# Four modulation vectors of layer 1 as VectorE sums in place of TensorE products

## The chip, the cores and the metric

The kernel runs on one core of a Trainium2 chip. Its time is the device time of one launch in microseconds (us), taken as the median of several executions. A separate execution was recorded by the hardware profiler; rows with times come from it. The engines are PE (TensorE, matrix products; PEld loads its stationary operands), DVE (VectorE), ACT (ScalarE), POOL (GpSimd) and SP (SyncE, which issues most DMAs). Each of them runs its own list of instructions in order, and semaphores tie the lists together.

## What is computed

Two layers over 512 latent tokens and 256 context tokens, D = 1024. Six modulation vectors per layer come from the condition `c` (and six from `c_ctx`); they shift, scale and gate the two halves of the layer:

```python
for layer in range(DEPTH):
    mod_x = silu_c @ ada_w[layer] + ada_b[layer]
    mod_c = silu_cc @ ada_w[layer] + ada_b[layer]
    sh1, sc1, g1, sh2, sc2, g2 = [m[:, None, :] for m in jnp.split(mod_x, 6, axis=-1)]
    ...
    hx = modulate(rmsnorm(x, norm1_g[layer]), sh1, sc1)
    ...
    x = x + g1 * (mx @ w_out[layer])
    hx = modulate(rmsnorm(x, norm2_g[layer]), sh2, sc2)
    x = x + g2 * squared_relu_mlp(hx, w_mlp1[layer], w_mlp2[layer])
```

The mixer that gives `mx` is four heads of bidirectional retention and four of gated linear attention behind one input projection; the output projection is `w_out`. Context tokens go through the same weights in layer 1.

## The kernel before, in words

**Products.** All float32 products of weights and activations are made of three float32r products (`mm3`, L437 to L439): high part by high part, high by low, low by high. A weight slab of 128 x 1024 comes by one DMA of 512 KB into one of four raw buffers (`NRAW = 4`), ACT makes its high part (L244), DVE its low part (L245), and up to `NSPL = 6` split slabs live at once. The raw buffers are shared by the slabs of the projections (`raw_wi`, `raw_wo`, `raw_wob`, `raw_m`) and the slabs of `ada_w` (`adaw`).

**What sets the order.** The program is a list of items. For the mixer it is written by hand in `SCHEDULE`, 25 lines, each with a projection block and the attention stages that run behind it. The items are emitted one after the other, and at each one `ch.tick()` emits the next step of every chain under way (norms, residuals, evacuations). No engine leaves this order afterwards.

**The modulation vectors.** Numbered u = 0 to 5 (sh1, sc1, g1, sh2, sc2, g2), 1024 features each, for two conditions. Layer 1's u = 0 and 1 are made on PE in quarters at the start. Its u = 2 to 5 are made on PE in 16 steps of `ada_step` (L279 to L292), in two groups g of 2048 features and eight k tiles each; one step stands after each slab block of `SCHEDULE`, from its first line on, until the 16 are done. A step loads two slabs and makes four fp32 products, 32 columns by 512. `ada_finish` then copies the rows out, transposes them on PE (four transposes of 128 x 128 per group) and adds the bias on DVE. Layer 2's six vectors are made another way, by `ada_sums` (L324 to L353), during layer 1's MLP: per k tile two DVE instructions, one per condition, add slab times scalar to a sum of 128 x 1024 (L340 for the first k tile, L342 for the other seven); after eight k tiles eight small products with a column of ones (L348) add up the partitions, and two transposes of 128 x 128 follow.

**The output projection of layer 1.** `wo0` to `wo7` for token group 0 (512 columns), then `wo6b`, `wo7b`, `wo0b`, ... in the order `second` for token group 1 (256 columns). In the traces their PSUM tiles are `pwo`, by the program's names pwo_j_g. After each, DVE adds the gated product to the residual stream `x` (L535), ACT squares it and DVE adds the square to the norm's sum (L473). While group 1 is projected, the second norm is applied to group 0: `xn` and `yl` on DVE (L517, L521, L515), `yh` on ACT, `xn` of two tiles on POOL (L510). Before the projection, `reload` lets POOL issue eight DMAs that bring `x` back into SBUF. The MLP follows.

Of the kernel before, what the change touches and what calls it, by code (L numbers as in the profile page):

```python
# [16 lines left out]
P = 128  # L17
# [22 lines left out]
class Item:  # L40
    """A piece of the program: emits instructions; may need weight slabs; a stage runs one block after its deps."""
# [5 lines left out]
class Chains:  # L47
    """Instruction chains that hop between engines: each tick emits the next step of every chain under way.

    Queued chains start one per tick, with at most WIDTH of them under way."""  # L50
# [45 lines left out]
class Act:  # L96
    """A moving operand in two float32r parts, made by chains for token ranges."""
# [10 lines left out]
# one block of projections and the attention stages that run behind it, per line; at most NSLOT tiles live  # L108
# [30 lines left out]
def build(ctx: ExitStack, tc, a):  # L139
# [7 lines left out]
    tp = ctx.enter_context(tc.tile_pool(name="tab", bufs=1))  # L147
    mp = ctx.enter_context(tc.tile_pool(name="mp", bufs=NSLOT))
# [23 lines left out]
    def bc(col, n):  # L172
        """[P, c] -> [P, c, n], each value repeated n times."""
        return col.rearrange("p (c o) -> p c o", o=1).to_broadcast([col.shape[0], col.shape[1], n])

    def rep(tab, c):
        """[P, n] -> [P, c, n], the row repeated c times."""
        return tab.rearrange("p (o t) -> p o t", o=1).to_broadcast([tab.shape[0], c, tab.shape[1]])
# [5 lines left out]
    # ---- constants and inputs  # L184
# [32 lines left out]
    # silu(c) of both vectors, as 32 stationary columns (30 of them zero) per k tile  # L217
# [14 lines left out]
    # ---- weight slabs: [128, 1024] and its exact split into two float32r parts  # L232
# [14 lines left out]
    class RankSlab(Slab):  # L247
        """Four copies of 32 columns per k tile: the second one's low part, the others' high parts."""
# [7 lines left out]
    # ---- adaLN vectors: mod[l][p, v, j] for feature 128 j + p  # L256
    mod = [const.tile([P, 2, 48], F32, name=f"mod{l}") for l in range(DEPTH)]

    def ada_finish(l, pt, tiles, n, fold=1):
        """pt: row 32 c + v holds, for vector v, n features from the tile tiles[c] on; `fold` such parts are summed."""  # L260
# [18 lines left out]
    def ada_step(state, l, g, kk):  # L279
        if kk == 0:  # L280
            state["pt"] = psa.tile([P, 512], F32, tag="psa", name=f"ada_{l}_{g}")
        pt = state["pt"]
        w = state.pop("w", None)
        if w is None:
            w = ada_load(l, g, kk)
        for c in range(4):
            nc.tensor.matmul(
                pt[32 * c : 32 * c + 32, :], cs[:, kk, :], w[c // 2][:, (c % 2) * 512 : (c % 2 + 1) * 512],
                start=(kk == 0), stop=(kk == KK - 1),
            )  # L290
        if kk == KK - 1:
            state["end", l, g] = ch.start(ada_finish(l, pt, [16 * g + 4 * c for c in range(4)], 512))  # L292

    def ada_load(l, g, kk):
        ws = []
        for i in range(2):
            w = wraw.tile([P, WCOL], F32, tag="raw", name=f"adaw_{l}_{g}_{kk}_{i}")
            c0 = g * 2048 + i * WCOL
            nc.sync.dma_start(w, a["ada_w"][l, kk * P : (kk + 1) * P, c0 : c0 + WCOL])
            ws.append(w)  # L300
        return ws

    ada_state = {}
    ada_queue = [(l, g, kk) for l, g in ((0, 1), (0, 2)) for kk in range(KK)]

    def ada_next():
        if ada_queue:
            l, g, kk = ada_queue.pop(0)
            ada_step(ada_state, l, g, kk)
            if ada_queue:  # L310
                ada_state["w"] = ada_load(*ada_queue[0])

    def ada_drain(l, g):
        while any(q[:2] == (l, g) for q in ada_queue):
            ada_next()
        ch.finish(ada_state["end", l, g])

    # the second layer's: weighted sums over the k tiles on the vector engine, one product to add the partitions
# [5 lines left out]
    def ada_sums(l):  # L324
        acc = tp.tile([P, 2, WCOL], F32, tag="rtab", name=f"adaacc_{l}")
        todo = [(u, kk) for u in range(6) for kk in range(KK)]
# [8 lines left out]
        for i, (u, kk) in enumerate(todo):  # L335
# [8 lines left out]
            if kk == KK - 1:  # L344
# [7 lines left out]
                ada_state["end", l] = ch.start(ada_finish(l, pt, [8 * u + 2 * c for c in range(4)], 256))  # L352
                yield  # L353

    # the first layer's shift and scale, in four quarters of 256 features each
# [18 lines left out]
    def quarter(q, middle=None, end=None):  # L374
        """Shift and scale of a quarter, even and odd k tiles apart."""
# [65 lines left out]
    def project(pt, slab, c0, acts, t0, t1, ks=None, first=0, last=None):  # L441
        """pt[:, :t1 - t0] += W[:, tile].T @ act over the k tiles `ks` of a slab part [kk, 128]."""
# [14 lines left out]
    # ---- RMSNorm over features, for a group of tokens at a time  # L457
    class Norm:
# [3 lines left out]
        def square(self, kk, t0, t1, first):  # L462
            """A chain that adds a tile's squares to the sum."""
# [14 lines left out]
        def late_square(self, kk, t0, t1):  # L478
            """A tile's squares that the product over the partitions adds to the sum."""
            sq = temp(f"sq_{self.name}_{kk}_{t0}")[:, 0 : t1 - t0]  # L480
            nc.scalar.activation(sq, xs[kk][:, t0:t1], AF.Square)
            self.late.append(sq)
# [40 lines left out]
        def apply_all(self, l, shift, v, t0, t1, ks=range(KK)):  # L523
            """Chains that make the tiles `ks` of a group of tokens."""
# [910 lines left out]
```

## Time and profile before

| what | us |
|---|---|
| median of 3 runs | 1659.86 (1658.58 to 1661.42) |
| span of the profiled execution (no other time of it is recorded) | 1658.9 |
| PE busy | 1618.7 (98%) |
| DVE busy | 946.9 (57%) |
| ACT busy | 629.5 (38%) |
| POOL busy | 201.6 (12%) |

A busy share says how full an engine's own list is, not who waits for whom. That is read from the waits (which engine stood idle, until what ended) and from the timeline, which gives the start of each instruction, its duration and in brackets how long its engine stood idle before it, and on which producer. Matmuls are pipelined, so their durations overlap; what one costs is read from the distance between starts.

### The profile page before, as it was taken

Reading aid. Unit: us, or ns where it says so; the run is one execution under the profiler, and the core shown is the slowest. Engines: PE = TensorE matmul, PEld = TensorE weight load, DVE = VectorE, ACT = ScalarE, POOL = GpSimd, SP = SyncE. Lnnn points to the kernel's source line nnn. Section 1 sums busy time; section 2 is a strip of 40 time slices with the busy share of each in tenths; the row PEclk is TensorE's granted clock in tenths of the full one; section 3 lists DMA queues with packets and bytes.
Section 4 is the critical chain, followed back from the end, with each engine's and each line's share of the span. In section 5 each row is a group of like instructions: output and inputs, shape, how many; then the busy total and the mean of one; then the engine's idle time right before and its main releaser. Section 6 shows DMA issues by size and latency. Waiting matters only on the chain. (4 is left out here: it accounts for less than half of the span.)

```text
span 1658.9 us, 22890 instructions
## 1 busy us (share of the span) xinstructions
PE 1618.7 (98%) x9236; PEld 1384.2 (83%) x9236; DVE 946.9 (57%) x1491; ACT 629.5 (38%) x1083; POOL 201.6 (12%) x215
## 2 busy tenths in 40 slices
PE   5999999999999999999999999999999899999997
PEld 3778888888998888888888887888889888888887
DVE  5676664554755555555556476588466633443445
ACT  5535424562532222222212246363464532222232
POOL 3200021110111010110101121001110211010010
PEclk9999999999999999999999999999999999999999
DMA  9533433122323333333333222121123323223321
GB/s 323 175 127 126 137 108 102 39 88 90 103 89 127 115 127 109 120 102 116 126 115 127 95 88 66 51 77 52 51 89 128 103 89 102 91 100 102 102 64 51
DMA packets 57610, 173.80 MB, mean 105 GB/s; under 512 B 6208, under 2 KB 17792, under 8 KB 57504
## 3 DMA queue, kind: packets, MB, share of 16 engines
q1 hardware_dynamic: 55232, 164.85, 30.2%
q0 software_dynamic: 2272, 7.50, 1.2%
q8 instruction: 72, 1.18, 0.3%
q14 instruction: 34, 0.28, 0.0%
HBM read 168.13 MB, written 4.19 MB: 104 GB/s over the span
## 5 line engine op out<-in xcount | busy, mean ns | idle before, releaser
L437 PE MATMUL pm<-yh,hi_m 128*128 128x512 f32 (+1 forms) x800 | 279.6, 349 | 0.0
L437 PE MATMUL pm<-hidh,hi_m 128*128 128x512 f32 (+1 forms) x800 | 279.1, 349 | 0.0
L438 PE MATMUL pm<-yl,hi_m 128*128 128x512 f32 (+1 forms) x800 | 278.6, 348 | 0.0
L438 PE MATMUL pm<-hidl,hi_m 128*128 128x512 f32 (+1 forms) x800 | 278.4, 348 | 0.0
L439 PE MATMUL pm<-yh,lo_m 128*128 128x512 f32 (+1 forms) x800 | 278.2, 348 | 0.0
L439 PE MATMUL pm<-hidh,lo_m 128*128 128x512 f32 (+1 forms) x800 | 277.2, 347 | 0.0
L1208 ACT ACTIVATE relu<-pm 128x512 f32<-128x512 f32 (+1 forms) x100 | 51.1, 511 | 497.6 <-PE pm L439 493.9
L1212 DVE TENSOR_TENSOR hidl<-relu,hidh 128x512 fp32r<-128x512 f32 (+1 forms) x100 | 60.5, 607 | 296.0 <-POOL relu L1210 296.0
L1210 POOL TENSOR_TENSOR relu<-relu 128x512 f32<-128x512 f32 (+1 forms) x100 | 89.2, 893 | 760.3 <-ACT hidh L1209 760.2
L535 DVE SCALAR_TENSOR_TENSOR x<-pm,mod,x 128x512 f32<-128x512 f32 (+1 forms) x200 | 117.6, 640 | 106.6 <-PE pm L439 106.6
L437 PEld LDWEIGHTS pm<-yh,hi_m 128*128 128x128 f32 x800 | 152.6, 191 | 20.2 <-issue 1.2
L437 PEld LDWEIGHTS pm<-hidh,hi_m 128*128 128x128 f32 x800 | 151.5, 189 | 21.3 <-issue 1.1
L438 PEld LDWEIGHTS pm<-yl,hi_m 128*128 128x128 f32 x800 | 152.5, 191 | 18.8
L439 PEld LDWEIGHTS pm<-yh,lo_m 128*128 128x128 f32 x800 | 152.4, 191 | 19.0
L439 PEld LDWEIGHTS pm<-hidh,lo_m 128*128 128x128 f32 x800 | 151.1, 189 | 19.6
L438 PEld LDWEIGHTS pm<-hidl,hi_m 128*128 128x128 f32 x800 | 151.4, 189 | 18.9 <-issue 0.2
L245 DVE TENSOR_TENSOR lo_m<-raw_m,hi_m 128x1024 fp32r<-128x1024 f32 x126 | 154.0, 1222 | 10.6 <-ACT hi_m L244 10.6
L244 ACT CAST hi_m<-raw_m 128x1024 fp32r<-128x1024 f32 x128 | 129.6, 1040 | 51.6 <-DMA raw_m<-in_w_mlp 31.0
L342 DVE SCALAR_TENSOR_TENSOR adaacc<-adaw,cs,adaacc 128x1024 f32<-128x1024 f32 x84 | 103.9, 1278 | 0.0
L245 DVE TENSOR_TENSOR lo_wi<-raw_wi,hi_wi 128x1024 fp32r<-128x1024 f32 x49 | 60.6, 1249 | 29.8 <-ACT hi_wi L244 29.8
L437 PE MATMUL pwo<-yh,hi_wo 128*128 128x256 f32 (+1 forms) x224 | 70.9, 316 | 0.1
L438 PE MATMUL pwo<-yl,hi_wo 128*128 128x256 f32 (+1 forms) x224 | 70.3, 314 | 0.3 <-DVE yl L1056 0.3
(304 smaller groups left out, 2951.5 us busy)
## 6 DMA issues: line engine op xcount, KB each, us to landing
raw_m<-in_w_mlp SPq DMA_DIRECT2D x128, 512.0 KB, 3.5
adaw<-in_ada_w SPq DMA_DIRECT2D x80, 512.0 KB, 3.9
raw_wi<-in_w_in SPq DMA_DIRECT2D x58, 512.0 KB, 4.3
adaw<-in_ada_w SPq DMA_DIRECT2D x32, 256.0 KB, 6.3
raw_wo<-in_w_out SPq DMA_DIRECT2D x16, 512.0 KB, 3.4
x<-in_xT POOLq DMA_DIRECT2D x8, 384.0 KB, 7.8
x<-in_xT SPq DMA_DIRECT2D x8, 256.0 KB, 4.9
raw_wob<-in_w_out SPq DMA_DIRECT2D x4, 512.0 KB, 4.3
```

The source lines that it names most:

```text
L244: nc.scalar.copy(self.hi, self.raw)
L245: self.engine.tensor_sub(self.lo, self.raw, f32(self.hi))
L342: nc.vector.scalar_tensor_tensor(acc[:, v], w, c, acc[:, v], op0=ALU.mult, op1=ALU.add)
L437: nc.tensor.matmul(out, wh, xh, start=first, stop=False)
L438: nc.tensor.matmul(out, wh, xl, start=False, stop=False)
L439: nc.tensor.matmul(out, wl, xh, start=False, stop=last)
L535: nc.vector.scalar_tensor_tensor(xs[kk][:, t0:t1], pt[:, 0 : t1 - t0], mod[l][:, v, gate + kk : gate + kk + 1], xs[kk][:, t0:t1], op0=ALU. ...
L1208: nc.scalar.activation(r, pt[:, 0 : t1 - t0], AF.Relu)
L1210: nc.gpsimd.tensor_mul(r, r, r)
L1212: nc.vector.tensor_sub(a_.lo[:, t0:t1], r, f32(a_.hi[:, t0:t1]))
```

## The change

The four vectors u = 2 to 5 of layer 1 are made by `ada_sums`, the way layer 2's are, and the 16 PE steps go. The sums of u = 2, 3 and 4 are emitted from the seventh line of `SCHEDULE` on, one k tile after each slab block and one at each line's end; the sum of u = 5, the gate of the MLP, one k tile after each of `wo4` to `wo7` and of the blocks of token group 1. The sum's accumulator gets a pool of its own (`adap`). The scratch space of POOL's own DMA descriptors is set to 2048 bytes. Comments and docstrings are blanked, so line numbers shift (L437 to L439 become L419 to L421, L342 becomes L306, L348 becomes L312). SP issues as many loads of `ada_w` as before, 512 KB each: one per k tile and vector in place of two per step.

```diff
+    adap = ctx.enter_context(tc.tile_pool(name="adap", bufs=1))
...
-    def ada_step(state, l, g, kk):
-        if kk == 0:
-            state["pt"] = psa.tile([P, 512], F32, tag="psa", name=f"ada_{l}_{g}")
...
-        for c in range(4):
-            nc.tensor.matmul(
-                pt[32 * c : 32 * c + 32, :], cs[:, kk, :], w[c // 2][:, (c % 2) * 512 : (c % 2 + 1) * 512],
-                start=(kk == 0), stop=(kk == KK - 1),
-            )
...
-    ada_queue = [(l, g, kk) for l, g in ((0, 1), (0, 2)) for kk in range(KK)]
...
-    def ada_sums(l):
-        acc = tp.tile([P, 2, WCOL], F32, tag="rtab", name=f"adaacc_{l}")
-        todo = [(u, kk) for u in range(6) for kk in range(KK)]
+    def ada_sums(l, us=range(6)):
+        acc = adap.tile([P, 2, WCOL], F32, tag="acc", name=f"adaacc_{l}")
+        todo = [(u, kk) for u in us for kk in range(KK)]
...
+    def ada_next(upto=5):
+
+        if "sums0" not in ada_state:
+            ada_state["sums0"] = [(u, ada_sums(0, [u])) for u in range(2, 6)]
+        while ada_state["sums0"] and ada_state["sums0"][0][0] <= upto:
+            try:
+                next(ada_state["sums0"][0][1])
+                return
+            except StopIteration:
+                ada_state["sums0"].pop(0)
...
-                if it.slabs and l == 0:
-                    plan.append(Item("ada", ada_next))
+                if it.slabs and l == 0 and ln > 5:
+                    plan.append(Item("ada", lambda: ada_next(4)))
+            if l == 0 and ln > 5:
+                plan.append(Item("ada", lambda: ada_next(4)))
...
                 if g == 0:
                     if l == 0:
-                        ada_drain(0, 2)
+                        ada_drain(4)
...
-            plan.append(Item("ada1", lambda: ada_drain(0, 1)))
+            plan.append(Item("ada1", lambda: ada_drain(2)))
...
             plan.append(Item(f"wo{j}", wo_part(j, korder, 0, wo[j]), [wo[j]]))
+            if l == 0:
+                plan.append(Item("ada", ada_next))
...
             plan.append(Item(f"wo{j}b", wo_part(j, korder, 1, s), [s]))
+            if l == 0:
+                plan.append(Item("ada", ada_next))
...
+                if l == 0 and u == 0 and jps == [0]:
+                    ada_drain(5)
...
-    nc = _bacc.Bacc("TRN2", target_bir_lowering=False, num_devices=1)
+    nc = _bacc.Bacc("TRN2", target_bir_lowering=False, num_devices=1, dynamic_dma_scratch_size=2048)
```

Where the instructions stand, on PE at the second block of token group 1 of the output projection (pwo_6_1 and pwo_7_1 are its first two blocks). Before:

```order
L437 MATMUL pwo_6_1_3785<-yh_4_3337,hi_wo_6_3457 128x256
L438 MATMUL pwo_6_1_3785<-yl_4_3338,hi_wo_6_3457 128x256
L439 MATMUL pwo_6_1_3785<-yh_4_3337,lo_wo_6_3458 128x256
L437 MATMUL pwo_7_1_3820<-yh_5_2765,hi_wo_7_3473 128x256
L438 MATMUL pwo_7_1_3820<-yl_5_2766,hi_wo_7_3473 128x256
L439 MATMUL pwo_7_1_3820<-yh_5_2765,lo_wo_7_3474 128x256
```

and in the changed kernel:

```order
L419 MATMUL pwo_6_1_3829<-yh_4_3341,hi_wo_6_3461 128x256
L420 MATMUL pwo_6_1_3829<-yl_4_3342,hi_wo_6_3461 128x256
L421 MATMUL pwo_6_1_3829<-yh_4_3341,lo_wo_6_3462 128x256
L312 MATMUL ada_5_3858<-adaacc_3530,onehot 32x256 x8
L419 MATMUL pwo_7_1_3869<-yh_5_2741,hi_wo_7_3477 128x256
L420 MATMUL pwo_7_1_3869<-yl_5_2742,hi_wo_7_3477 128x256
L421 MATMUL pwo_7_1_3869<-yh_5_2741,lo_wo_7_3478 128x256
```

Between the two blocks now stand the products of the sum of u = 5, which read the accumulator adaacc; before, PE went from one block to the next.

The same place on DVE (x_j<-pwo_j_1 is the residual of block j of group 1, yl_j the second norm of group 0, lo_m a slab's low part). Before:

```order
L521 SCALAR_TENSOR_TENSOR yl_4_3338<-xn_n_0_4_0_3733,mod_149,yh_4_3337 128x512
L517 SCALAR_TENSOR_TENSOR xn_n_0_6_0_3777<-x_6_3354,mods_n_0_3646,ssum_n_0_3453 128x512
L245 TENSOR_TENSOR lo_m_0_1_3782<-raw_m_0_1_3735,hi_m_0_1_3781 128x1024
L515 TENSOR_TENSOR yl_5_2766<-xn_n_0_5_0_3768,yh_5_2765 128x512
L517 SCALAR_TENSOR_TENSOR xn_n_0_7_0_3812<-x_7_3356,mods_n_0_3646,ssum_n_0_3453 128x512
L535 SCALAR_TENSOR_TENSOR x_6_3354<-pwo_6_1_3785,mod_149,x_6_3354 128x256
L473 TENSOR_TENSOR ssum_n_0_3453<-ssum_n_0_3453,sq_n_0_6_512_3815 128x256
L521 SCALAR_TENSOR_TENSOR yl_6_2991<-xn_n_0_6_0_3777,mod_149,yh_6_2990 128x512
L521 SCALAR_TENSOR_TENSOR yl_7_3257<-xn_n_0_7_0_3812,mod_149,yh_7_3256 128x512
L535 SCALAR_TENSOR_TENSOR x_7_3356<-pwo_7_1_3820,mod_149,x_7_3356 128x256
```

and in the changed kernel:

```order
L306 SCALAR_TENSOR_TENSOR adaacc_3530<-adaw_5_6_3724,cs,adaacc_3530 128x1024 x2
L503 SCALAR_TENSOR_TENSOR yl_4_3342<-xn_n_0_4_0_3760,mod_152,yh_4_3341 128x512
L499 SCALAR_TENSOR_TENSOR xn_n_0_6_0_3783<-x_6_3358,mods_n_0_3673,ssum_n_0_3457 128x512
L497 TENSOR_TENSOR yl_5_2742<-xn_n_0_5_0_3768,yh_5_2741 128x512
L499 SCALAR_TENSOR_TENSOR xn_n_0_7_0_3812<-x_7_3360,mods_n_0_3673,ssum_n_0_3457 128x512
L517 SCALAR_TENSOR_TENSOR x_5_3356<-pwo_5_1_3785,mod_152,x_5_3356 128x256
L455 TENSOR_TENSOR ssum_n_0_3457<-ssum_n_0_3457,sq_n_0_5_512_3815 128x256
L503 SCALAR_TENSOR_TENSOR yl_6_2991<-xn_n_0_6_0_3783,mod_152,yh_6_2990 128x512
L246 TENSOR_TENSOR lo_m_0_1_3823<-raw_m_0_1_3770,hi_m_0_1_3822 128x1024
L306 SCALAR_TENSOR_TENSOR adaacc_3530<-adaw_5_7_3776,cs,adaacc_3530 128x1024 x2
L503 SCALAR_TENSOR_TENSOR yl_7_3261<-xn_n_0_7_0_3812,mod_152,yh_7_3260 128x512
L517 SCALAR_TENSOR_TENSOR x_6_3358<-pwo_6_1_3829,mod_152,x_6_3358 128x256
```

The last two k tiles of u = 5 now stand among the norm of group 0, ahead of the residual of x_6; the products on PE above wait for the last of them, adaacc with adaw_5_7. The first six (adaw_5_0 to adaw_5_5) stand farther up, three ahead of the residual x_7 of group 0 and three behind it. In the same way the last k tile of u = 2 stands on DVE behind the row gk_3 of the fourth gated head, and its products on PE behind the last matmul of ps_ka_0_512, where a step of the second group stood before.

## Rows read from the trace of the kernel before

**Rows 1.** the page, part 1: busy us, share of span, number of instructions

```profile
PE 1618.7 (98%) x9236; PEld 1384.2 (83%) x9236; DVE 946.9 (57%) x1491; ACT 629.5 (38%) x1083; POOL 201.6 (12%) x215
```

**Rows 2.** busy time by window: stretch; busy us and instructions of PE, PEld, DVE, ACT, POOL; PEclk, DMA

```profile
400.00:450.00 50.00, 50.00 (x310) 44.71 (x309) 31.33 (x46) 23.36 (x36) 3.69 (x4) 1.00 0.22 71
```

**Rows 3.** timeline of PE: start, us, engine, line, operation, tiles, in brackets idle before

```profile
87.75 0.39 PE L438 MATMUL ps_vg<-lo_wi,hh_n 128*128 128x512 f32 x1
87.97 0.39 PE L439 MATMUL ps_vg<-hi_wi,hl_n 128*128 128x512 f32 x1
88.29 1.06 PE L287 MATMUL ada<-adaw,cs 128*32 128x512 f32 x8
89.29 0.50 PE L437 MATMUL ps_vg<-hi_wi,hh_n 128*128 128x512 f32 x1
89.62 0.39 PE L438 MATMUL ps_vg<-lo_wi,hh_n 128*128 128x512 f32 x1
```

**Rows 4.** timeline of PE in layer 1's MLP, around one sum's product for layer 2

```profile
544.45 0.28 PE L439 MATMUL pm<-hidh,lo_m 128*128 128x256 f32 x1
544.65 1.07 PE L348 MATMUL ada<-adaacc,onehot 128*32 128x256 f32 x16
545.65 0.50 PE L437 MATMUL pm<-yh,hi_m 128*128 128x512 f32 x1
```

**Rows 5.** timeline of DVE in layer 1's MLP, one pair of running sums

```profile
488.13 2.47 DVE L342 SCALAR_TENSOR_TENSOR adaacc<-adaw,cs,adaacc 128x1024 f32<-128x1024 f32 x2
490.52 1.22 DVE L245 TENSOR_TENSOR lo_m<-raw_m,hi_m 128x1024 fp32r<-128x1024 f32 x1
```

**Rows 6.** timeline of DVE along the output projection of layer 1

```profile
411.41 0.75 DVE L535 SCALAR_TENSOR_TENSOR x<-pwo,mod,x 128x512 f32<-128x512 f32 x1 [3.25 <-PE pwo L439]
...
414.29 0.48 DVE L535 SCALAR_TENSOR_TENSOR x<-pwo,mod,x 128x256 f32<-128x256 f32 x1 [0.68 <-PE pwo L439]
416.19 1.23 DVE L245 TENSOR_TENSOR lo_wob<-raw_wob,hi_wob 128x1024 fp32r<-128x1024 f32 x1 [1.42 <-ACT hi_wob L244]
...
433.53 1.23 DVE L245 TENSOR_TENSOR lo_m<-raw_m,hi_m 128x1024 fp32r<-128x1024 f32 x1 [0.74 <-ACT hi_m L244]
...
435.94 0.48 DVE L535 SCALAR_TENSOR_TENSOR x<-pwo,mod,x 128x256 f32<-128x256 f32 x1
...
437.24 1.41 DVE L521 SCALAR_TENSOR_TENSOR yl<-xn_n,mod,yh 128x512 fp32r<-128x512 f32 x2
```

**Rows 7.** timeline of PE, the first product of pwo_7_1

```profile
426.45 0.28 PE L437 MATMUL pwo<-yh,hi_wo 128*128 128x256 f32 x1
```

**Rows 8.** timeline of DVE along the third and fourth gated heads (173 to 196 us)

```profile
173.26 1.02 DVE L789 SCALAR_TENSOR_TENSOR gq<-gq,c_glag,gt 128x768 f32<-128x768 f32 x1 [10.17 <-ACT gt L784]
...
193.61 1.07 DVE L861 COPY_PREDICATED gt<-maskb,psb 128x512 f32<-128x512 uint8 x2 [2.59 <-ACT gt L860]
...
195.43 0.95 DVE L836 TENSOR_TENSOR gk<-gk,gl 128x768 f32<-128x768 f32 x1
```

**Rows 9.** timeline of PE, the ada step after ps_ka_0_512

```profile
202.50 1.06 PE L287 MATMUL ada<-adaw,cs 128*32 128x512 f32 x8
```

**Rows 10.** waits of PE over the whole span: us in total, times, longest

```profile
PE psf L857 <- DVE gk L836: 1.0, 1, 1.0
...
PE po L903 <- DVE gl L893: 0.6, 1, 0.6
```

**Rows 11.** timeline of PE at the last norm's statistics of layer 2

```profile
1297.16 1.22 PE L490 MATMUL st_n<-ssum_n,ones_d 128*128 128x256 f32 x2 [4.43 <-DVE ssum_n L473]
```

**Rows 12.** busy time by window after that wait (columns as in rows 2)

```profile
1297.00:1303.00 6.00, 5.84 (x26) 5.66 (x27) 5.20 (x8) 3.02 (x7) 2.19 (x3) 0.53 0.54 176
```

**Rows 13.** timeline of POOL, the reload and the output projection

```profile
365.61 4.28 POOL L1165 DMA_DIRECT2D x<-in_xT  x8 [45.28 <-PE ps_g L438]
...
417.49 1.29 POOL L510 TENSOR_TENSOR xn_n<-x,ssum_n 128x512 f32<-128x512 f32 x1 [47.60 <-DVE mods_n L499]
```

**Rows 14.** the page, part 6: DMA issue, KB each, median us to landing

```profile
x<-in_xT POOLq DMA_DIRECT2D x8, 384.0 KB, 7.8
```

More of the change, by code (lines that the diff above doesn't have):

```diff
@@ L277, in ada_finish @@
             )
-    def ada_step(state, l, g, kk):
-        if kk == 0:
-            state["pt"] = psa.tile([P, 512], F32, tag="psa", name=f"ada_{l}_{g}")
[L282 to L285, printed above, removed]
-        for c in range(4):
-            nc.tensor.matmul(
-                pt[32 * c : 32 * c + 32, :], cs[:, kk, :], w[c // 2][:, (c % 2) * 512 : (c % 2 + 1) * 512],
-                start=(kk == 0), stop=(kk == KK - 1),
-            )
[L291 to L301, printed above, removed]
-    ada_state = {}
-    ada_queue = [(l, g, kk) for l, g in ((0, 1), (0, 2)) for kk in range(KK)]
[L306 to L316, printed above, removed]
+    ada_state = {}
     onehot = const.tile([P, 2, 32], F32, name="onehot")
@@ L351, in ada_sums, with ada_drain @@
                         )
-                ada_state["end", l] = ch.start(ada_finish(l, pt, [8 * u + 2 * c for c in range(4)], 256))
+                ada_state["end", l] = ada_state["end", l, u] = ch.start(
+                    ada_finish(l, pt, [8 * u + 2 * c for c in range(4)], 256)
+                )
                 yield
+    def ada_next(upto=5):
[7 more added lines that the diff above has]
+                ada_state["sums0"].pop(0)
+    def ada_drain(u):
+        while (0, u) not in [k[1:] for k in ada_state if k[0] == "end" and len(k) == 3]:
+            ada_next(u)
+        ch.finish(ada_state["end", 0, u])
     QF = 256
@@ L1123, in layer @@
         seen = {"d", "gq0", "gk0"}
-        for line in SCHEDULE.split("\n")[1:-1]:
+        for ln, line in enumerate(SCHEDULE.split("\n")[1:-1]):
             row = line.split()
```

## The prediction

> **What bounds the kernel now.** I read the busy shares first: PE 1618.7 of 1658.9 us, DVE 946.9 [rows 1]. The page does not say whether PE is full where the change works, so I looked at the ten windows from 60 to 550 us, of 50 us each but the first; all have PE busy throughout. The one along the output projection: PE busy for all of its 50.00 us at a granted clock of 1.00, DVE for 31.33 [rows 2]. So in the mixer and the projection of layer 1 PE's own list sets the time: a microsecond taken off it, or put on it as a wait, moves the end by one, and no later idle time on PE there gives it back. DVE looks free for 37% of that window. Whether it is free at the right moment is not in a share; it is read from DVE's timeline against the place where PE comes to need the result.
>
> **What the change takes off PE.** One old step: neighbours follow each other at 0.23 us (87.75 to 87.97, rounded up); from the matmul at 87.97 to the one behind the step at 89.29 it is 1.32, so the step costs 1.09 [rows 3]. The next matmul starts 0.33 later (89.62) in place of 0.23, which is 0.10 more; not every step has such a neighbour, so I take 1.15 with bounds of 1.09 and 1.20. Sixteen steps: 18.4 (17.4 to 19.2). Their eight transposes of 128 x 128 are replaced by eight others of the same size: nothing.
>
> **What it puts on PE.** The product of one sum in the MLP: the matmul at 544.45 has 256 columns, half of those at 87.75, so the next could start half of 0.23 later, at 544.57, and the next one starts at 545.65 [rows 4]: 1.08. Four of them, with some 0.1 in all: 4.4. PE's list alone becomes 18.4 - 4.4 = **14.0 us shorter** (13.0 to 14.8).
>
> **What it puts on DVE.** A pair of running sums takes 2.39 (488.13 to 490.52) [rows 5] and a vector has eight of them (the first, without an addition, I take as no longer): 19.1, four vectors 76 us, on an engine with some 18 us free in each 50 [rows 2]. On average they fit. Two places do not look like the average.
>
> **The gate of the MLP along the output projection.** Here is the largest term. PE's product for u = 5 stands between pwo_6_1 and pwo_7_1, and needs the last pair of its sum. PE comes there where pwo_7_1 now begins, at 426.45 [rows 7]. I follow DVE in the order of the new kernel, with the durations of the old one. The first three pairs fall into gaps in which DVE waits for PE; the last such gap is the 3.25 us before the residual at 411.41 [rows 6], longer than a pair. From 411.41 to the end of the second-to-last yl (437.24 plus half of 1.41, so 437.9) DVE needs 26.5 in the old order. The residual of x_6 and its sum, 435.94 to 437.24, now stand behind: 25.2. Five pairs come in: 5 x 2.39 = 11.95. They fill those gaps in which DVE waits for something that doesn't itself wait for DVE, 0.68 at 414.29 and 0.74 at 433.53; the others (1.42 at 416.19 and four of 0.48) are DVE, then ACT, then DVE again, and stay. So the last pair ends at 411.41 + 25.2 + 11.95 - 1.42 = 447.1, and PE waits 447.1 - 426.45 = **20.7 us**. If all seven gaps, 4.75 in sum from 0.68 to 0.74, were filled, it would be 17.4. Both ends shift alike with what PE saved earlier, since the residual at 411.41 itself waited for PE. That DVE is behind PE here already in the old kernel is the plain sign: it begins the residual of x_6 at 435.94 [rows 6], 9.5 us after PE was done with that block. That lag cost nothing, since nobody needed its result soon; the change puts a product at PE's place that does. Behind that product the rest of the projection and the whole MLP are queued.
>
> POOL's part of the norm may stretch this: two POOL instructions of 1.29 run in this stretch, the first at 417.49 [rows 13]. If DVE stood still for both, 2 x 1.29 = 2.6 would come on top; no row shows a running sum beside POOL, so the sum takes none and the range all of it. The Trainium skill, "SBUF — State Buffer", section "Who interferes with whom", says that a DVE instruction with two SBUF inputs contends with a GpSimd instruction that reads SBUF, and a running sum has two such inputs; by that rule the total below would be up to 2.6 higher, without it as it stands.
>
> **The sum of u = 2 at the fourth gated head.** DVE works from 173.26, after a gap of 10.17 that hides what comes before, to the end of gk_3 at 195.43 + 0.95 = 196.38, idle for 2.59 [rows 8] and once for under half a microsecond, 3.0 together. The new order puts the last five pairs of u = 2 into this stretch or right behind it: 196.38 + 11.95 - 3.0 = 205.3. PE comes to the product at 202.50 [rows 9] less two removed steps of this stretch, 200.3. PE waits **5.0 us** (2.5 to 5.0: the low end if DVE starts a pair earlier, in that first gap).
>
> **Smaller waits.** PE now comes up to some 4 us earlier to the mixer's stages, which wait for DVE and ACT. Layer 2's mixer has the same schedule without steps between its blocks, and PE waits there 1.0 for gk and 0.6 for gl [rows 10]: I take **1.6** (0 to 5).
>
> **The clock.** After a wait of 4.43 us in layer 2 [rows 11], the granted clock is 0.53 over the 6 us from 1297 to 1303, in which PE is busy [rows 12], so it works most of them at the lower of its two levels, 1.2 in place of 2.4 GHz. That costs 6 x 0.47 = 2.8 us. The two long waits above are at least about as long as this one: 2 x 2.8 = **5.6** (2.8 if the shorter one leaves the clock as it is).
>
> **DMA.** SP issues as many loads of the same size, later ones. Each waits for a raw buffer that DVE freed one or two pairs earlier, so I put them at nothing; if they came late, DVE would be late too, which only lengthens the waits above. The smaller scratch for POOL's descriptors concerns the eight transfers that reload x, 7.8 us each to landing [rows 14].
>
> **Sum.** 1658.9 - 14.0 + 20.7 + 5.0 + 1.6 + 5.6 = 1677.8 for the profiled execution. The median is 1659.86, 0.96 above that execution's span, so the forecast is **1678.8 us**, about 19 slower. Low end: 1658.9 - 14.8 + 17.4 + 2.8, with the other waits at nothing, is 1664.3, so 1665. High end: 1658.9 - 13.0 + 23.3 + 5.0 + 5.0 + 5.6 = 1684.8, so 1686.
>
> **Rivals.**
>
> *A, the sums are hidden.* Layer 2's six sums lie behind the MLP in the old kernel, and PE goes from the neighbour at 544.45 straight into their product [rows 4]. If DVE's spare time [rows 2] covers layer 1's as well, no wait comes in and the kernel is 1658.9 - 14.0 + 0.96 = 1645.9. It decides by when DVE ends the last pair of u = 5: before 426.45 of the old clock. Against it stands that DVE is 9.5 us behind PE there without any sum. The Trainium skill, "Perfetto Trace Analysis", section "Identifying the Most-Contended Engine", says to relieve the engine with the highest occupancy; by that rule work moved from PE to DVE should pay, and the trace agrees on the shares but not on this place. Chance 0.08. The break-even lies where waits and clock together come to 14 us.
>
> *B, half of the wait.* If DVE's chains fit together better than in my walk, say the wait of u = 5 is half (10.3 with 2.8 for the clock), u = 2 comes in time and the small waits stay: 1658.9 - 14.0 + 10.3 + 2.8 + 1.6 + 0.96 = 1660.6, no change that a measurement can tell. For it speaks only that DVE's order in the MLP and the projection is interleaved by many chains; against it that even all gaps filled leave 17.4. Chance 0.05.
>
> *C, the reload becomes serial.* If the smaller scratch made each of POOL's eight transfers wait for the one before, the last x, issued from 365.61 on [rows 13], would land at 365.61 + 8 x 7.8 = 428.0 [rows 14]; its residual stands at 411.41 [rows 6], so up to 16.6 us would come on top: 1695. Nothing in the trace shows what the scratch bounds. Chance 0.03.
>
> *That the change does not do what it says* is left out: the new order shows the sums, the products and no step on PE.
>
> **How the numbers follow.** Forecast 1678.8 with 0.82, nearly all of it between 1665 and 1686; A 0.08, B 0.05, C 0.03, something not seen 0.02. The range of 1665 to 1686 leaves out A, B and C, under 2 in 10. A measurement of this kernel tells 0.2%, 3.3 us, from no change. Faster by that: A, 0.08, and a little of B, 0.09. Within it: 0.05. Slower: 0.86.
>
> **What would show it.** In the changed kernel's waits of PE: one row of some 20 us for the product of u = 5 on the running sum, one of some 5 us for u = 2, none of note for u = 3 and 4. In the windows: a granted clock near 0.5 for some microseconds behind each, and PE idle along the output projection where it was full. In DVE's timeline: no idle time over 1.5 us between the residual x_7 of group 0 and the last pair of u = 5. Wrong it would be if PE's product of u = 5 followed pwo_6_1 without a wait (then A), or if DVE stood idle before the residuals for a DMA of x (then C).

## The result, and the profile after

The changed kernel takes 1683.28 us (median, 1683.12 to 1683.40) beside 1659.85 for the kernel before: ratio 1.0140, 95% interval 1.0127 to 1.0152. The profiled execution has a span of 1681.4, so 22.5 us more than the one before. The forecast was 1678.8 in a range of 1665 to 1686.

The waits of PE in the changed kernel (us in total, times, longest), without those at the program's start:

```profile
PE ada L312 <- DVE adaacc L306: 27.5, 4, 20.4
...
PE adat L269 <- ACT adarow L264: 2.1, 3, 1.1
...
PE ps_g L419 <- DVE sg L1029: 1.4, 1, 1.4
PE psf L839 <- DVE gk L818: 1.3, 2, 1.0
PE ps_vr L420 <- DVE lo_wi L246: 1.0, 1, 1.0
```

The first row is new: the products of the sums wait 27.5 us for DVE, 20.43 of them for u = 5 and 4.36 for u = 2. Of psf's 1.3, 1.0 were there before [rows 10].

The waits for u = 2, and for u = 3, which waits for one sum after the other:

```profile
197.08 2.28 PE L312 MATMUL ada<-adaacc,onehot 128*32 128x256 f32 x16 [4.36 <-DVE adaacc L306]
...
257.85 0.64 PE L312 MATMUL ada<-adaacc,onehot 128*32 128x256 f32 x8 [0.59 <-DVE adaacc L306]
260.60 0.64 PE L312 MATMUL ada<-adaacc,onehot 128*32 128x256 f32 x8 [2.12 <-DVE adaacc L306]
```

The large wait on PE's timeline, the last matmul of pwo_6_1, the product of u = 5 and the first of pwo_7_1:

```profile
426.47 0.28 PE L421 MATMUL pwo<-yh,lo_wo 128*128 128x256 f32 x1
447.18 2.28 PE L312 MATMUL ada<-adaacc,onehot 128*32 128x256 f32 x16 [20.43 <-DVE adaacc L306]
449.39 0.58 PE L419 MATMUL pwo<-yh,hi_wo 128*128 128x256 f32 x1
```

And DVE's timeline there, from the residual of x_7 to the last pair and the residual of x_6 (compare [rows 6]):

```profile
411.55 0.75 DVE L517 SCALAR_TENSOR_TENSOR x<-pwo,mod,x 128x512 f32<-128x512 f32 x1 [0.86 <-PE pwo L421]
...
419.09 3.52 DVE L306 SCALAR_TENSOR_TENSOR adaacc<-adaw,cs,adaacc 128x1024 f32<-128x1024 f32 x2
...
422.80 1.42 DVE L499 SCALAR_TENSOR_TENSOR xn_n<-x,mods_n,ssum_n 128x512 f32<-128x512 f32 x2
...
445.85 2.48 DVE L306 SCALAR_TENSOR_TENSOR adaacc<-adaw,cs,adaacc 128x1024 f32<-128x1024 f32 x2
448.24 0.75 DVE L503 SCALAR_TENSOR_TENSOR yl<-xn_n,mod,yh 128x512 fp32r<-128x512 f32 x1
448.90 0.48 DVE L517 SCALAR_TENSOR_TENSOR x<-pwo,mod,x 128x256 f32<-128x256 f32 x1
```

Windows (columns as in [rows 2]): the gated heads, the output projection, and the clock within and behind the wait.

```profile
150.00:200.00 50.00, 45.27 (x288) 38.16 (x288) 47.09 (x62) 23.50 (x44) 3.96 (x4) 0.95 0.39 119
400.00:450.00 50.00, 29.45 (x192) 25.12 (x191) 40.95 (x50) 16.18 (x25) 3.55 (x2) 0.80 0.38 120
430.00:440.00 10.00, 0.00 (x0) 0.00 (x0) 9.06 (x12) 4.22 (x6) 0.00 (x0) 0.52 0.44 150
446.00:450.00 4.00, 2.71 (x19) 1.02 (x20) 3.52 (x5) 0.59 (x2) 0.00 (x0) 0.50 0.53 177
450.00:452.00 2.00, 2.00 (x15) 2.00 (x15) 0.29 (x1) 0.09 (x1) 0.00 (x0) 0.80 0.44 174
```

PE, full in the old projection [rows 2], is busy for 29.45 of 50 us. DVE is busy for 47.09 and 40.95 us of the two windows of 50.

To see where time came and went I matched the matmuls of the two executions and took start after minus start before (negative: PE is ahead of the old kernel):

| matmul (start before) | difference, us | what lies in the stretch above it |
|---|---|---|
| psf of the third head (191.80) | -9.91 | ten steps and four transposes gone, waits of 1.0 and 0.3 |
| psf of the fourth head (203.49) | -4.20 | one step gone, wait of 4.36 for u = 2, product at the lower clock |
| ps_kb_1 (264.26) | -3.09 | the last five steps gone; lower clock, product and waits of 0.6 and 2.1 for u = 3 |
| hs of the fourth retention head (328.12) | +0.16 | wait of 1.45 for a PSUM bank that DVE still reads, product of u = 4, wait of 1.1 for its rows |
| first of pwo_7_1 (426.45) | +22.94 | product and wait of 20.43 for u = 5 |
| the last ones (1649.86) | +22.45 | some lower clock behind the wait, given back in layer 2 |

So the gain was real: 9.9 us by 191.80. All of it, and what the last six steps would have added, was spent on three products and the waits around them before the output projection began, and the fourth put the whole loss on top. Of the differences, 0.72 us stand already at 59.83, ahead of the first removed step: PE was that much later there in this execution. In the other kernels with sums (section below) this start differs from the old one by -1.3 to +0.9 us.

### The profile page after: what moved, and what is told of

Read it like the earlier page. It is cut to its first block, busy times and chain, and to the rows that moved or that the text cites. A ratio compares the mean times of both kernels' runs of the same rounds, so it can differ in the third digit from the quotient of the medians.

```text
span 1681.4 us, 22850 instructions
## 1 busy us (share of the span) xinstructions
PE 1608.8 (96%) x9172; PEld 1384.3 (82%) x9172; DVE 1026.2 (61%) x1563; ACT 629.9 (37%) x1085; POOL 206.8 (12%) x215
## 5 line engine op out<-in xcount | busy, mean ns | idle before, releaser
L419 PE MATMUL pm<-yh,hi_m 128*128 128x512 f32 (+1 forms) x800 | 279.7, 350 | 0.0
L419 PE MATMUL pm<-hidh,hi_m 128*128 128x512 f32 (+1 forms) x800 | 279.3, 349 | 0.0
L421 PE MATMUL pm<-yh,lo_m 128*128 128x512 f32 (+1 forms) x800 | 278.2, 348 | 0.0
L421 PE MATMUL pm<-hidh,lo_m 128*128 128x512 f32 (+1 forms) x800 | 277.5, 347 | 0.0
L306 DVE SCALAR_TENSOR_TENSOR adaacc<-adaw,cs,adaacc 128x1024 f32<-128x1024 f32 x140 | 183.4, 1352 | 0.2
L419 PEld LDWEIGHTS pm<-yh,hi_m 128*128 128x128 f32 x800 | 152.5, 191 | 20.3 <-issue 1.2
L419 PEld LDWEIGHTS pm<-hidh,hi_m 128*128 128x128 f32 x800 | 151.5, 189 | 21.2 <-issue 1.1
L421 PEld LDWEIGHTS pm<-yh,lo_m 128*128 128x128 f32 x800 | 152.3, 190 | 19.0
L421 PEld LDWEIGHTS pm<-hidh,lo_m 128*128 128x128 f32 x800 | 151.3, 189 | 19.5
L246 DVE TENSOR_TENSOR lo_wi<-raw_wi,hi_wi 128x1024 fp32r<-128x1024 f32 x49 | 60.5, 1249 | 20.5 <-ACT hi_wi L245 20.4
L419 PE MATMUL ps_g<-hh_n,hi_wi 128*128 128x512 f32 (+1 forms) x192 | 70.6, 367 | 1.4 <-DVE sg L1029 1.4
L419 PE MATMUL pwo<-yh,hi_wo 128*128 128x256 f32 (+1 forms) x224 | 71.3, 319 | 0.1
```

Source lines behind the costliest of these rows:

```text
L246: self.engine.tensor_sub(self.lo, self.raw, f32(self.hi))
L306: nc.vector.scalar_tensor_tensor(acc[:, v], w, c, acc[:, v], op0=ALU.mult, op1=ALU.add)
L419: nc.tensor.matmul(out, wh, xh, start=first, stop=False)
L421: nc.tensor.matmul(out, wl, xh, start=False, stop=last)
```

## Experiments

Ratios are to the kernel before, with 95% intervals.

**The scratch alone.** The kernel before with one edit:

```diff
-    nc = _bacc.Bacc("TRN2", target_bir_lowering=False, num_devices=1)
+    nc = _bacc.Bacc("TRN2", target_bir_lowering=False, num_devices=1, dynamic_dma_scratch_size=2048)
```

> The kernel before with the smaller scratch for POOL's DMA descriptors as its only edit. Theory (the scratch does not bound the reload or the loads at the start): 1659.9 us, within 0.5 us of the kernel before. Rival (transfers issued by POOL wait for one another): over 1663 us, with later landings of x at the reload.

Measured: 1660.04 us, 0.9997 (0.9988 to 1.0006). The scratch costs nothing; rival C is out.

**Sums of one k tile.** PE's list is that of the changed kernel, DVE makes only the first pair of each vector:

```diff
-            w, nxt = nxt, load(i + 1) if i + 1 < len(todo) else None
-            for v in range(2):
+            if l == 0 and kk:
+                nxt = None
+            else:
+                w, nxt = nxt, load(i + 1) if l and i + 1 < len(todo) else None
+            for v in range(0 if l == 0 and kk else 2):
```

> The changed kernel with the running sums of layer 1 cut to their first k tile (the other seven loads and DVE pairs of each of the four vectors left out), PE's list unchanged. Theory (PE's own list is 14 us shorter, all the rest of the loss is waits for DVE): no wait of PE on a running sum, 1645 to 1648 us. Rival (part of the loss is not DVE's: the scratch, the pool, or PE's new products themselves): above 1652 us.

Measured: 1656.95 us, 0.9979 (0.9970 to 0.9989), so the theory's range (1645 to 1648) was missed by 9 us, and the time is on the rival's side, for a reason that neither names. No product waits for a sum, and at 426.45 of the old clock PE is 13.05 us ahead: the price of PE's list was right. But then PE waits for ACT. PE and ACT of this kernel:

```profile
412.40 1.07 PE L315 MATMUL ada<-adaacc,onehot 128*32 128x256 f32 x16
424.63 0.69 PE L269 MATMUL adat<-c_ident,adarow 128*128 128x128 f32 x2 [8.10 <-ACT adarow L264]
```

```profile
423.90 0.42 ACT L456 ACTIVATE sq_n<-x 128x256 f32<-128x256 f32 x1 [2.35 <-DVE x L520]
424.22 0.35 ACT L264 COPY adarow<-ada 128x256 f32<-128x256 f32 x1
```

ACT's copy of the product's rows stands behind the square of x_6, which waits for DVE's residual of x_6, the one that was 9.5 us late in the old kernel [rows 6, 7]. PE's transposes wait 8.10 for it, and 2 to 3 us of low clock follow. So even a sum that costs DVE next to nothing, one pair of eight, loses most of the gain at this place. In the changed kernel this wait is hidden behind the longer one.

**The gate's sum in the MLP.** One pair after each of the first eight MLP products:

```diff
             if u:
                 plan.append(Item("ada", mlp_ada))
+            elif l == 0:
+                plan.append(Item("ada", ada_next))
```

(and no `ada_next` along the output projection).

> The changed kernel, with the sum of u = 5 one stage later: its eight k tiles follow the eight first MLP products of unit 0, its product stands ahead of the first use of the gate. Theory (PE waits because DVE is busy with the second norm at that place): the wait of 20.4 us and some 1.7 us of low clock behind it go, up to 3 us come back where the last pair is late for the product: 1661 to 1664 us. Rival (the DVE work itself is too much for layer 1, and any place shows it): the wait moves with the sum, 1678 to 1683 us.

Measured: 1679.59 us, 1.0112 (1.0097 to 1.0127). The theory said 1661 to 1664; the rival had it. PE now waits at the product in the MLP, and loses 3.3 us more just ahead of it, between 426.45 and 459.88 of the old clock, in short waits for the second norm of group 1:

```profile
484.27 2.28 PE L312 MATMUL ada<-adaacc,onehot 128*32 128x256 f32 x16 [13.12 <-DVE adaacc L306]
```

**Only the product later.** DVE's order as changed, PE's product of u = 5 at the first use of the gate:

```diff
-            if l == 0:
+            if l == 0 and i < 4:
                 plan.append(Item("ada", ada_next))
```

> The changed kernel with DVE's order as it is, and only PE's product of u = 5 moved from the output projection to the first use of the gate in the MLP. Theory A (the running sums also make the second norm late): PE then waits at the first MLP product for the last yl tiles, which end at 444 and 449 us in the changed kernel, where PE would need them by about 441: some 9 us of wait with 1 to 2 us of low clock in place of 20.4 and 1.7, so about 1671 us. Theory B (only the place of the product costs, the norm has room): 1661 us.

Measured: 1674.52 us, 1.0082 (1.0062 to 1.0102), nearer to theory A (1671) than to B (1661), and 3.5 us over A. The wait for the sum became waits for the norm that DVE makes between the pairs:

```profile
441.56 0.50 PE L420 MATMUL pm<-yl,hi_m 128*128 128x512 f32 x1 [1.65 <-DVE yl L503]
...
446.31 0.80 PE L420 MATMUL pm<-yl,hi_m 128*128 128x512 f32 x1 [3.78 <-DVE yl L503]
```

**The gate's sum directly behind that of u = 4**, before and among the first blocks of the projection:

```diff
-                    plan.append(Item("ada", lambda: ada_next(4)))
+                    plan.append(Item("ada", ada_next))
```

(the same at the lines' ends).

> The changed kernel with the sum of u = 5 begun directly behind that of u = 4 instead of at the fifth block of the output projection; its last pair then stands among the first four blocks of the projection, where the trace of the changed kernel has DVE busy for 28.6 of 50 us. Theory (what costs is the place along the second norm, not the amount of DVE work): the wait of 20.4 us and the 1.7 us of low clock behind it go, at most 1 us comes back: 1660 to 1663 us. Rival (the work does not fit into layer 1 wherever it stands, as the move into the MLP suggests): a wait of 10 us or more at the product, 1672 us or more.

Measured: 1681.57 us, 1.0121 (1.0099 to 1.0143): the rival again.

```profile
385.55 2.28 PE L312 MATMUL ada<-adaacc,onehot 128*32 128x256 f32 x16 [13.99 <-DVE adaacc L306]
```

The four executions lie between 1676.62 and 1684.38, and the profiled one is among the long ones: some 3 us of its time went ahead of the projection, where low clock followed a wait that cost none in the changed kernel (last section).

This refutes my theory that the place along the norm makes the whole wait. Three places gave waits of 20.4, 13.1 and 14.0. Common to them is that eight pairs, some 18 us of DVE, begin 20 to 32 us of PE's time ahead of the product, and that the product stands directly behind the last pair. The old trace tells what the place does add. Its DVE instructions ahead of the last pair behind u = 4 and in the MLP, and PE's matmuls at the places of the two products:

```profile
371.15 0.42 DVE L1047 TENSOR_TENSOR sg<-se,ps_g 128x256 f32<-128x256 f32 x1 [0.48 <-ACT se L1046]
...
471.06 0.42 DVE L1212 TENSOR_TENSOR hidl<-relu,hidh 128x256 fp32r<-128x256 f32 x1 [1.98 <-POOL relu L1210]
```

```profile
367.67 0.40 PE L437 MATMUL pwo<-yh,hi_wo 128*128 128x512 f32 x1
...
469.31 0.40 PE L437 MATMUL pm<-hidh,hi_m 128*128 128x512 f32 x1
```

So without any sum DVE ends the work that stands ahead of the last pair 3.8 us (371.5) and 2.1 us (471.4) after PE is at the product's place, and along the norm 10.2 us (437.9 less 1.3, against 426.45) [rows 6, 7]. Taken off the three waits, this leaves 10.2 along the norm, 11.0 in the MLP and 10.2 behind u = 4: nearly the same each time. Half of the wait along the norm is DVE's old lag there, the other half pairs that found no gap. The free time of DVE in the old trace does not tell this: between the first pair and PE's arrival it is 13.7, 5.4 and 13.7 us.

**Short POOL instructions.** The addition that ends the rotation and one of two decay products cut short in layer 1, which leaves out part of both (the decay product is cut to one chunk of six; that part of the edit is not shown):

```diff
-                            nc.gpsimd.tensor_add(dst[i][:, 0:LAT], dst[i][:, 0:LAT], w)
+                            nq_ = 32 if l == 0 else LAT
+                            nc.gpsimd.tensor_add(dst[i][:, 0:nq_], dst[i][:, 0:nq_], w[:, 0:nq_])
```

> The changed kernel with two of POOL's operations in layer 1's mixer cut short: the addition that ends the rotation does 32 of 512 columns, and one of the two decay products per head does one chunk of six, so part of the rotation and of the decay is left out. Theory (a running sum beside a POOL instruction is stretched, and this makes the waits for u = 2 and 3): the pairs that took 3.5 to 4.7 us go back to 2.4 to 2.5 where POOL's work is gone, PE's waits for u = 2 and 3 shrink from 4.4 and 2.7 to about 3.4 and under 0.5 us, the time by 3 to 5 us, to 1678.5 to 1680.5. Rival (the pairs are long for another reason, such as DMA or PSUM): pairs and time unchanged, 1683.3.

Measured: 1678.76 us, 1.0108 (1.0093 to 1.0123), 4.5 under the changed kernel. Pairs of u = 3 on DVE's timeline, changed kernel:

```profile
214.79 3.51 DVE L306 SCALAR_TENSOR_TENSOR adaacc<-adaw,cs,adaacc 128x1024 f32<-128x1024 f32 x2
...
230.23 4.07 DVE L306 SCALAR_TENSOR_TENSOR adaacc<-adaw,cs,adaacc 128x1024 f32<-128x1024 f32 x2
...
255.86 4.68 DVE L306 SCALAR_TENSOR_TENSOR adaacc<-adaw,cs,adaacc 128x1024 f32<-128x1024 f32 x2
```

and the same three with POOL cut short:

```profile
213.75 2.48 DVE L306 SCALAR_TENSOR_TENSOR adaacc<-adaw,cs,adaacc 128x1024 f32<-128x1024 f32 x2
...
228.16 2.82 DVE L306 SCALAR_TENSOR_TENSOR adaacc<-adaw,cs,adaacc 128x1024 f32<-128x1024 f32 x2
...
251.59 2.48 DVE L306 SCALAR_TENSOR_TENSOR adaacc<-adaw,cs,adaacc 128x1024 f32<-128x1024 f32 x2
```

All product waits but that of u = 5 fall from 27.5 - 20.4 = 7.1 to 24.3 - 20.4 = 3.9 us: u = 2 from 4.36 to 3.30 and 0.56 for its second sum, u = 3 from 2.7 to none. The theory holds; u = 2 gained less than it said.

**Products one step later.** The gate behind u = 4 as above, and one more step (`yield`) ahead of each product:

```diff
             if kk == KK - 1:
+                for _ in range(1 if l == 0 else 0):
+                    yield
                 pt = psa.tile([P, 512], F32, tag="psa", name=f"ada_{l}_{u}")
```

> As the kernel with the gate behind u = 4, and PE's product of each sum one step later than its last pair. Theory (the products of u = 2 to 4 wait since they stand directly behind the last pair on an engine that runs late): the waits of 4.4, 2.7 and the low clock of 2.5 us behind the first go, the waits of 1.1 for rows and 1.4 for a bank stay: 1651 to 1655 us. Rival (DVE is so late in the gated heads that other work of PE waits in their place): 1658 us or more.

Measured: 1661.56 us, 1.0007 (0.9998 to 1.0017). No product waits, 22 us of the loss are gone, and still more than 6 us are missing to the theory (1651 to 1655), so the rival had it: other work of PE now waits, 3.3 us for gk in the fourth head, and 2.9 us behind ACT and DVE in the projection, after which the granted clock is 0.50 from 382 to 388, some 3 us more:

```profile
382.12 0.80 PE L421 MATMUL pwo<-yh,hi_wo 128*128 128x512 f32 x1 [2.90 <-ACT yh L1038]
```

**The same from the third line on** (`ln > 1` in place of `ln > 5`).

> As the one with the products deferred, and the sums begun at the third line of the schedule instead of the seventh, where DVE has some 20 us free in 50 and POOL is idle. Theory (DVE has room there): waits of PE on running sums under 1 us in all, 1648 to 1653 us. Rival (DVE, in order, comes late for the first gated heads instead): PE waits for gk or gl, over 1655 us.

Measured: 1667.63 us, 1.0040 (1.0025 to 1.0055): the rival. PE is only 5.2 us ahead at the third head (10.7 in the one before), with waits for gk, for gl and for ACT's rows. About 1 us of the difference is the product of u = 2, which now stands ahead of that head; nothing behind makes up for the rest.

**A slower pace.** One pair after each slab block from the first line on, one more at four lines' ends and behind the first four parts of the projection, two accumulators, each product two steps behind its last pair (part of the edit):

```diff
-                if it.slabs and l == 0 and ln > 5:
-                    plan.append(Item("ada", lambda: ada_next(4)))
-            if l == 0 and ln > 5:
-                plan.append(Item("ada", lambda: ada_next(4)))
+                if it.slabs and l == 0 and ln >= 0 and ln not in ():
+                    plan.append(Item("ada", ada_next))
+            if l == 0 and ln in (11, 13, 15, 17):
+                plan.append(Item("ada", ada_next))
```

> The four vectors as sums with one pair per step at a slower pace: one k tile after each slab block from the schedule's first line on, one more at four lines' ends and behind the first four parts of the output projection, two accumulators, and each product two steps behind its last pair (u = 5 ahead of the seventh block of token group 0). Theory (what decides is how much DVE work stands in each stretch of PE's time and that no product follows its last pair directly): no wait of PE on a running sum over 1 us, low clock at none or one place, 1648 to 1656 us. Rival (DVE, even so, comes late for the gated heads, where the decay chain goes back and forth between DVE, ACT and PE): psf and po wait, 1658 us or more.

Measured: 1659.20 us, 0.9999 (0.9990 to 1.0008): 24 us better than the changed kernel, no change against the old one. The time is that of the rival (1658 or more), but not for the rival's reason, since psf does not wait and po only 0.5 us. With the same 32 pairs on DVE no product waits any more; that part of the theory holds. PE's waits from 60 to 500 us:

```profile
PE adat L269 <- ACT adarow L264: 4.2, 2, 3.1
PE ps_vr L454 <- DVE lo_wi L246: 3.4, 1, 3.4
PE ps_g L453 <- DVE sg L1063: 1.9, 2, 1.4
PE po L919 <- DVE gl L909: 0.5, 1, 0.5
```

**Without pairs at the heads' decays** (`ln not in (3, 4, 9, 10)`, eight line ends from 12 to 19). The expectation names five lines; the edit leaves the third with its pair, so four go without: the fourth, fifth, tenth and eleventh.

> As the paced one, but without pairs at the five lines of the schedule in which DVE makes the decays of the gated heads (lines 3 to 5, 10 and 11), with pairs at more line ends behind them. If DVE's lateness in the gated heads is what remains of the loss, the waits for gk and gl there shrink against the paced one and the time falls by 1 to 4 us; if it is not, the time stays within 1 us of the paced one, or rises where the pairs now stand closer (lines 13 to 20).

Measured: 1665.18 us, 1.0032 (1.0020 to 1.0045): slower. The waits in the heads hardly changed (0.8 for the rotation, 0.5 for gl); the row for ACT's copy grew to 6.2 us where the pairs now stand closer. So taking these pairs away gained nothing, and the gated heads are not what is left of the loss.

**Transposes later.** The paced one with ACT's copy and the transposes seven steps apart in place of two, and no pair at the first three lines:

```diff
-        yield
-        yield
+        for _ in range(7 if l == 0 and tiles[0] >= 16 else 2):
+            yield
         tt = bank(f"adat_{l}_{tiles[0]}")
```

> As the paced kernel, with three edits: the transposes behind each product of u = 2 to 5 come seven steps after ACT's copy of the rows in place of two, the first three slab blocks have no pair, and the last pairs stand behind the fifth and sixth block of the output projection. Theory (in the paced kernel PE lost 4.2 us in two waits for ACT's copy of the rows, 3.4 us and its low clock at the weights that DVE splits by 104 us, both a matter of place): these rows shrink to under 1.2 us each, and the time to 1649 to 1653 us, faster than the kernel before. Rival (the copy waits on ACT for as long as DVE is late, wherever the transposes stand): the waits stay and the time too, 1657 to 1661.

Measured: 1659.53 us, 0.9998 (0.9989 to 1.0007), in the rival's range. PE is 15.2 us ahead at 275.62 of the old clock and still 8.7 at 371.32. Then one wait takes most of it, with the low clock behind it:

```profile
368.08 0.69 PE L269 MATMUL adat<-c_ident,adarow 128*128 128x128 f32 x2 [4.76 <-ACT adarow L264]
```

**The same with 14 steps.**

> As the paced kernel with late transposes, and the transposes 14 steps behind ACT's copy in place of 7. In that kernel one wait was left, 4.8 us for ACT's copy of the rows of u = 4 at 363 us, and 2 to 3 us of low clock behind it; up to there PE was 8.7 us ahead of the kernel before. Theory (a matter of place): that wait goes, PE keeps some 8 us: 1651 to 1654 us. Rival (another wait for ACT or DVE takes its place in the output projection, since both run late there): 1657 to 1660 us.

Measured: 1662.13 us, 1.0008 (0.9999 to 1.0017): the rival, 2 us above its range. That wait is gone, and the product of u = 5 waits in its place, first for one and then for the other of its two sums:

```profile
409.47 0.64 PE L335 MATMUL ada<-adaacc,onehot 128*32 128x256 f32 x8 [4.59 <-DVE adaacc L362]
...
410.66 0.66 PE L335 MATMUL ada<-adaacc,onehot 128*32 128x256 f32 x4 [0.56 <-DVE adaacc L362]
```

No version that computes the whole output beat the kernel before by more than the measurement tells. What stays open: in three kernels (steps deferred by one, transposes by 7 and by 14) PE came to the output projection 6 to 9 us ahead (at 371.32 of the old clock) and lost it there, each time on another row, for ACT's copy, ACT's yh or DVE's sum. That points at the work that ACT and DVE hand to each other between 330 and 410 us as the limit of that stretch; no run took that work away, so it is argued, not shown. Nor was a sum tried on another engine than DVE, or only some of the four vectors moved.

## Why the prediction was right, and where its terms were off

- **PE's list, -14.0.** Right. The kernel with sums of one k tile was 13.05 us ahead at the place of u = 5, after a wait of 1.0, though it was 0.3 late at the start.
- **The wait for u = 5, 20.7.** Measured 20.43. The mechanism was right: DVE's lag and five pairs in its order, without a gap over 1.42 us. That the number fits to 0.3 us is in part luck. The walk let the last pair end at 447.1; it ended at 448.24, 1.0 later once the 0.14 is taken off by which the residual of x_7 itself moved. But PE's product needs only the first sum of that pair to start, and started at 447.18; the two errors cancel. POOL cost nothing on balance: a pair beside it took 3.52 (419.09), but the two xn behind, which had met POOL before (2.39 for both at 417.61 in the old trace), took 1.42. The Trainium skill, "SBUF — State Buffer", section "Who interferes with whom", says that a DVE instruction with two SBUF inputs contends with a GpSimd instruction that reads SBUF. The trace agrees with that for the pair, but the 2.6 us by which the high end of the range allowed for it (an estimate, two POOL instructions of 1.29) did not come on top, because one DVE instruction took the other's place beside POOL.
- **The reason given for it** was half of the matter. I took the lag of DVE along the second norm for the cause. It is 10.2 us of the wait; the other 10.2 come with eight pairs at one per step wherever they were put that close (11.0 and 10.2 at the two other places). The paced kernel shows that no product waits for the 32 pairs when they stand farther apart and the products later.
- **The wait for u = 2, 5.0.** Measured 4.36. Here too PE started on the first sum of the last pair, 1.1 us ahead of the pair's end (197.08 against 195.75 + 2.39 = 198.14).
- **The clock, 5.6.** Too much by about a quarter. Behind u = 2 the product took 2.21 us (197.08 to 199.29) in place of 1.08, and the following products of the head lost about as much again, some 2.3 together. Behind u = 5 the product took 2.21 as well, and six matmuls 0.09 more each, some 1.7. In sum 4, since the low level ended 3.5 us after PE's restart at 447.18, where I had reckoned 6 us [rows 12].
- **Smaller waits, 1.6.** This is the term that was mis-sized. Measured: 1.0 (ps_vr), 0.3 (psf), 2.7 (u = 3, in two parts), 1.45 (a bank), 1.1 (rows of u = 4): 6.6. I took layer 2's mixer for the nearest row, which has no sums in it. I said that nothing of note would wait for u = 3; its pairs were stretched beside POOL by up to 2.2 us each, and shortening POOL's work took that wait away. The price of POOL was weighed at the wrong place: POOL works 12.09 of 50 us in the changed kernel's window from 200 to 250, and 3.55 along the projection. The rule of the Trainium skill cited above bears on that window.
- **The sum.** -14.0 + 20.4 + 4.4 + 4.0 + 6.6 = 21.4 of the 22.5 us by which the spans differ. Of the rest of 1.1, 0.72 are the later start at 59.83, ahead of the first removed step; 0.4 I can't place. The terms that came out too high (u = 2 and clock, 2.2 together) hide part of the 5.0 by which the smaller waits came out too low.
- **Rival A (1645.9).** It did not come, and could not have with the products at these places: without any sum on DVE beyond the first pair the kernel takes 1656.95, since ACT's copy of the rows stands behind DVE's late residuals. I had priced the product and left its follow-up on ACT and PE out. The Trainium skill, "Perfetto Trace Analysis", section "Identifying the Most-Contended Engine", says to optimize the engine with the highest occupancy first, and to judge TensorE by its weight loads or its share of peak rather than by its matmuls' busy time. By the shares of this trace that is PE either way (98%, PEld 83%, DVE 57%) [rows 1], but taking work off it onto DVE gained nothing in any of the ten kernels that compute the whole output with sums, the changed one included.
- **Rivals B and C.** Neither came. For B, DVE's chains did not fit together better than in the walk; the scratch of C was shown to cost nothing.

## What to carry to other kernels

Work moved from a full engine to a half-full one can pay only if it fits stretch by stretch, and here even the version in which it fits gained nothing. The free time of the receiving engine over the stretch is not enough to tell: 18 us of pairs met 13.7 us of free time in two places and waits of 14 and 20 us came of it, since DVE was 4 and 10 us late there already and most gaps are shorter than a pair. What told it was a walk along the receiving engine's list, starting from how late that engine already is, up to the instruction that the full engine needs. Place the consumer several steps behind the last piece, and follow the result through every engine that handles it (here DVE, PE, ACT, PE, DVE): the copy that stands behind a late engine's work cost 8.10 us of wait where the sum itself was nearly gone.

## What the runs showed of the hardware that was not expected

- Running sums with two operands in SBUF and POOL's additions lengthen each other: a pair took 3.51 beside POOL in place of 2.48, and POOL's two additions 3.72, as this row of the changed kernel shows, in place of 2.66 in the old one:

```profile
213.50 3.72 POOL L928 TENSOR_TENSOR rk<-rk,rw_k 128x512 f32<-128x512 f32 x2 [21.14 <-ACT rk L913]
```

- In these runs the loss of clock does not grow with the wait. After 20.43 us of waiting the granted clock was back at 1.00 some 4 us after the restart, after 4.43 us in the old kernel [rows 11, 12] it took longer. Nor does the length of a wait tell whether the clock falls at all: the second wait of u = 3 lasted 2.12 us in the changed kernel and in the one with the gate behind u = 4, and the 4 us behind it ran at 1.00 in the first and at 0.50 in the second (the wait in the second kernel, then both windows, columns as in [rows 2]):

```profile
261.35 1.08 PE L312 MATMUL ada<-adaacc,onehot 128*32 128x256 f32 x8 [2.12 <-DVE adaacc L306]
```

```profile
260.60:264.60 4.00, 4.00 (x23) 2.98 (x24) 2.23 (x3) 1.32 (x2) 0.00 (x0) 1.00 0.42 131
261.30:265.30 4.00, 3.96 (x15) 2.59 (x16) 2.25 (x3) 1.32 (x2) 0.00 (x0) 0.50 0.40 131
```

  The wait for gk in the fourth head did the same: the granted clock was 1.00 behind 3.27 us of it in the kernel with the products one step later, and 0.50 behind 3.28 us in the one from the third line on.
- A product of eight matmuls of 32 x 256 on sums costs PE 1.08 us, as much as one old step of four matmuls of 32 x 512: what the change saves is the number of them, 4 in place of 16.
